# Splitting the first two experts' biases ahead of time, and moving the first norm's scale and shift into the first expert's product

## The chip, the cores and the metric

The kernel runs on one core of one Trainium2 chip. The metric is the device time of one execution, in microseconds (us). A core has five engines that run their own instruction streams in order: PE (matrix products), DVE (vector), ACT (activation), POOL and SP (which here only issues DMAs). Sixteen DMA engines move data between HBM and the on-chip memory.

## The reference, cut to what matters

One layer: an RWKV-7 time mixer, a norm, a mixture of 32 experts with four of them per token, a second norm, a gated per-layer input, a third norm. 256 tokens, width 1024, all in float32. The part around the change:

```
x = layer_norm(ALPHA * x + mixed, ln_mix_g, ln_mix_b)         # first norm: scale g, shift b
logits = x @ router_w + router_b;  top 4 of 32, softmax        # router
h = x_e @ w_gu[e] + b_gu[e]                                    # 1024 -> 2048, for each expert e
act = min(h[:F], 7) * sigmoid(1.702 * ...) * (clip(h[F:]) + 1)
y_e = act @ w_down[e] + b_down[e]                              # 1024 -> 1024
x = layer_norm(ALPHA * x + sum of gated y_e, ln_ffn_g, ln_ffn_b)
```

Each expert has 8 MB of `w_gu` and 4 MB of `w_down`, so the experts read 403 MB of weights.

## The kernel before

**Stages.** `rwkv` (the mixer), `route` (first norm without its scale and shift, router, one-hot matrices, gathering of the first two experts' tokens into `xg0`), `overflow` (four products that clear the output sums `acc`, and a branch that all engines take together), `experts`, `tail`.

**The ring.** Expert weights stream through a ring of eleven 2 MB tiles. A plan lists them in order: for each pair of experts eight `gu` tiles (four an expert, two of eight k steps each), then four `d` tiles. Eleven are issued before the experts begin. After that `ring.free` puts the next load of the plan into a tile as soon as PE has read it for the last time; SP issues these loads in that order (L128 for `gu`, L139 for `d`).

**Order of the experts.** For pair b: `gu(2b)`, `gu(2b+1)` (products `ph`, L1215, then the bias, L1222), `combine` of the pair before, `tr` (transposes, L1235), `gates`, for even b `gather` (products `pg`, L1188, for the next four experts), `down` (`pd`, L1263). PE's order is that of the code between `step()` calls and the scheduler's inside one; DVE's and ACT's order is the scheduler's throughout. `bank` hands out four PSUM banks for all of these products.

**The biases.** `biases` loads all 32 experts' biases in six pieces of 512 columns, each into 96 rows of a scratch tile (three copies of 32 rows, L1049), and splits each into three bf16 parts in `B3`: two casts on ACT (L1051, L1053), two subtractions (L1052, L1054) and a cast (L1055) on DVE. A one-column selector then adds expert e's bias to a sum with one matmul for each 512 columns.

**First norm's scale and shift.** `residual`, between `gu(0)` and `gu(1)`, spreads g and b over the partitions with four matmuls (`pgb`, L1200), applies them to `x1` on DVE (L1202), and adds ALPHA * x1 to `acc` with the matrix `scaled` (L1204).

Of the kernel before, what the change touches and what calls it, by code (L numbers as in the profile page):

```python
# [16 lines left out]
OP = mybir.AluOpType  # L17
# [154 lines left out]
def consts(tc, pool):  # L172
    nc = tc.nc
    c = {}
    ident = pool.tile([128, 128], F32, name="ident")
    nc.gpsimd.memset(ident, 1.0)
    nc.gpsimd.affine_select(ident, ident, pattern=[[1, 128]], compare_op=OP.is_equal, fill=0.0,
                            base=0, channel_multiplier=-1)
    c["ident"] = ident
    identr = pool.tile([128, 128], F32R, name="identr")  # L180
    nc.scalar.copy(identr, ident)
    c["identr"] = identr
    upto = pool.tile([128, 128], F32, name="upto")
    nc.gpsimd.memset(upto, 1.0)
    nc.gpsimd.affine_select(upto, upto, pattern=[[1, 128]], compare_op=OP.is_ge, fill=0.0,
                            base=0, channel_multiplier=-1)
    c["upto"] = upto
    ones = pool.tile([128, 128], F32, name="ones")
    nc.gpsimd.memset(ones, 1.0)
    c["ones"] = ones  # L190
    iota = pool.tile([128, CAP], F32, name="iota")
    nc.gpsimd.iota(iota, pattern=[[1, CAP]], base=1, channel_multiplier=0, allow_small_or_imprecise_dtypes=True)
    c["iota"] = iota
    scaled = pool.tile([128, 128], F32, name="scaled")
    nc.gpsimd.tensor_scalar(scaled, ident, ALPHA, None, op0=OP.mult)
    c["scaled"] = scaled
    return c


# [801 lines left out]
class Moe:  # L1001
    def __init__(self, tc, keep, c, A, x1):
        self.tc, self.c, self.A, self.x1 = tc, c, A, x1
        self.gate = keep.tile([128, 2, E], F32, name="gate")
        self.pos = keep.tile([128, 2, E], F32, name="pos")
        self.cnt = keep.tile([128, E + 1], I32, name="cnt")
        self.pm = keep.tile([128, 2, KC], F32, name="pm")

    def first(self, pool):

# [3 lines left out]
    def prepare(self, RP, ps):  # L1014
# [6 lines left out]
        for i, nm in enumerate(["ln_mix_g", "ln_mix_b"]):  # L1021
# [14 lines left out]
        nc.vector.scalar_tensor_tensor(rw, pc[:, 0:E][:, None, :].to_broadcast([128, KC, E]), -1.0 / D, rw,  # L1036
                                       op0=OP.mult, op1=OP.add)

    def biases(self, W, scratch):

        nc, A, ident = self.tc.nc, self.A, self.c["ident"]
        B3 = W.tile([96, 3 * D], BF, name="B3")
        sel3 = W.tile([96, E], BF, name="sel3")
        n = 512
        for i, bf in enumerate(scratch):
            bf = bf[0:96]
            src = A["moe_b_gu"] if i * n < 2 * D else A["moe_b_down"]
            cols = i * n % (2 * D)
            nc.sync.dma_start(bf, bass.AP(tensor=src.tensor, offset=src.offset + cols, ap=[[0, 3], [src.shape[-1], E], [1, n]]))  # L1049
            o = B3[:, i * n:i * n + n]  # L1050
            nc.scalar.copy(o, bf)  # L1051
            nc.vector.tensor_sub(bf[0:64], bf[0:64], o[0:64])  # L1052
            nc.scalar.copy(o[0:64], bf[0:64])  # L1053
            nc.vector.tensor_sub(bf[32:64], bf[32:64], o[32:64])  # L1054
            nc.vector.tensor_copy(o[32:64], bf[32:64])  # L1055
        for r in range(3):
            rs = slice(32 * r, 32 * r + 32)
            nc.gpsimd.tensor_scalar(sel3[rs, :], ident[rs, rs], 1.0, 0.0, op0=OP.mult, op1=OP.add)
        return B3, sel3

    def route(self, RP, psA, psB, psI, sums):

# [72 lines left out]
    def experts(self, ring):  # L1135
# [4 lines left out]
        with ExitStack() as ctx:  # L1140
# [24 lines left out]
            def bank(name):  # L1165
                return PS.tile([128, 512], F32, name=name, tag="m", bufs=4)

            def one(e):
                return sel3[:, e:e + 1].to_broadcast([96, CAP])

            def batch(e):

# [5 lines left out]
            def gather(e):  # L1178
# [4 lines left out]
                for q in range(KC // 2):  # L1183
# [6 lines left out]
                    copy = nc.vector.tensor_copy if q % 2 else nc.scalar.copy  # L1190
                    copy(xq[:, 2 * q:2 * q + 2, 0:n * CAP], pg[:, :, 0:n * CAP])

            def residual():

                for i, op in enumerate((OP.mult, OP.add)):
                    for h in range(2):
                        hs = slice(512 * h, 512 * h + 512)
                        pb = bank("pgb")
                        r = 32 * h
                        nc.tensor.matmul(pb, ident[r:r + 2, r + i:r + i + 1].to_broadcast([2, 128]), rows[h], start=True, stop=True)  # L1200
                        for cp in range(2):
                            nc.vector.tensor_tensor(x1[cp][:, hs], x1[cp][:, hs], pb, op=op)  # L1202
                            if i:
                                nc.tensor.matmul(acc[cp][h], c["scaled"], x1[cp][:, hs], start=False, stop=False,  # L1204
                                                 skip_group_check=True)

            def gu(e):
                xg, _, i = batch(e)
                ph = [bank(f"ph{n}") for n in range(2)]
                for k in range(KC):  # L1210
                    w = ring["gu", e, k // 2]
                    for n in range(2):
                        for h in range(2):
                            o = n * D + h * 512
                            pe(nc.tensor.matmul(ph[n][64 * h:64 * h + 64, :], xg[:, k, i * CAP:i * CAP + CAP],  # L1215
                                                w[:, k % 2, o:o + 512], start=k == 0, stop=False))
                    if k % 2:
                        ring.free(("gu", e, k // 2))
                for n in range(2):
                    for h in range(2):  # L1220
                        o = n * D + h * 512
                        pe(nc.tensor.matmul(ph[n][64 * h:64 * h + 64, :], one(e), B3[:, o:o + 512], start=False, stop=True))  # L1222
                step()
                s = act[e % 2]
                nc.vector.tensor_scalar(g, ph[0], 7.0, None, op0=OP.min)  # L1225
                nc.vector.tensor_scalar(l, ph[1], 7.0, -7.0, op0=OP.min, op1=OP.max)
                nc.scalar.activation(s, g, AF.Sigmoid, scale=1.702)  # L1227
                nc.vector.scalar_tensor_tensor(l, l, 1.0, g, op0=OP.add, op1=OP.mult)
                nc.vector.tensor_mul(s, s, l)
# [20 lines left out]
            def down(b):  # L1250


                pd = [bank(f"pd{h}") for h in range(2)]
                for i in range(2):
                    e = 2 * b + i
                    side = [slice(64 * (i ^ h), 64 * (i ^ h) + 64) for h in range(2)]
                    for h in range(2):
                        o = 2 * D + 512 * h
                        pe(nc.tensor.matmul(pd[h][side[h], :], one(e), B3[:, o:o + 512], start=True, stop=False))  # L1259
                    for fh in range(2):  # L1260
                        for k in range(4):
                            for h in range(2):
                                pe(nc.tensor.matmul(pd[h][side[h], :], actT[:, i, k, 64 * fh:64 * fh + 64],  # L1263
                                                    ring["d", e, fh][:, k, 512 * h:512 * h + 512],
                                                    start=False, stop=fh == 1 and k == 3))
                        ring.free(("d", e, fh))
                    step()
                nc.scalar.copy(ob[:, 0], pd[0])  # L1268
                for i in range(2):
                    nc.vector.tensor_copy(ob[64 * i:64 * i + 64, 1], pd[1][64 - 64 * i:128 - 64 * i])  # L1270
# [5 lines left out]
                                            start=False, stop=2 * b == E - 2, skip_group_check=True))  # L1276
                    step()

            rows = [act[1][32 * h:32 * h + 2] for h in range(2)]
            for h in range(2):  # L1280
                for i, nm in enumerate(["ln_mix_g", "ln_mix_b"]):
                    nc.sync.dma_start(rows[h][i:i + 1], self.A[nm][:, 512 * h:512 * h + 512])
            B3, sel3 = self.biases(W, [ob[:, 0], ob[:, 1], g, l] + [xq[:, 2 * i:2 * i + 2].rearrange("p a b -> p (a b)") for i in range(2)])
            ring.rest()
            for b in range(E // 2):
                gu(2 * b)
                if not b:
                    residual()
                gu(2 * b + 1)
                if b:  # L1290
                    combine(b - 1)
                self.ready(ring, bank, b - READY, pe)
                step()
                tr(2 * b)
                pgt = gates(b)
                nc.vector.tensor_copy(GT, pgt[:, 0:T])
                if b % 2 == 0 and b < E // 2 - 1:
                    gather(2 * b + 2)
                    step()
                tr(2 * b + 1)  # L1300
                down(b)
# [237 lines left out]
```

## Time and profile before

| | |
|---|---|
| median of 3 runs | 1335.9 us (1335.29 to 1336.46) |
| the profiled execution's own time | 1339.56 us |
| its span, first to last instruction | 1337.9 us |
| PE busy | 1213.4 us (91%) |
| DVE, ACT, POOL busy | 440.4, 216.8, 178.3 us |
| mean granted TensorE clock | 0.952 of full speed |
| mean DMA traffic | 323 GB/s |

The stages lie in the span so: the mixer and `route` to 346 us, the experts from 347 to 1289 us, the tail to 1338 us. "Share" in DMA columns is the mean busy share of the 16 DMA engines; "<-" names what an engine waited for.

### The profile page before, as it was taken

How to read it: one execution, taken by the hardware profiler on the slowest of the kernel's cores; microseconds unless marked ns; L12 is line 12 of the kernel's file. 1: busy time of each engine (PE TensorE's matmuls, PEld its weight loads, DVE VectorE, ACT ScalarE, POOL GpSimd, SP SyncE). 2: the span in 40 equal slices, each digit the busy share in tenths (PEclk: the TensorE clock that was granted, in tenths of full speed). 3: DMA queues.
4: the chain of work that ended last, by engine and by line, in shares of the span. 5: the costliest groups of instructions: out<-in, count | busy, mean ns of one | idle time of the engine just before them, and what ended most of it. 6: DMA issues, size and time to landing. Idle time of an engine off the chain costs nothing.

```text
span 1337.9 us, 14931 instructions
## 1 busy us (share of the span) xinstructions
PE 1213.4 (91%) x5983; PEld 693.4 (52%) x5984; DVE 440.4 (33%) x1080; ACT 216.8 (16%) x459; POOL 178.3 (13%) x308
## 2 busy tenths in 40 slices
PE   6988888988789999999988988999899989989996
PEld 5666666776326545645634432554255345525642
DVE  5886879885231112111102011111111111101235
ACT  3544434441211001000000000101010010101001
POOL 9465646530000000000000000000000000000000
PEclk9987879896879999999999999999999999999988
DMA  7331101475469999999999899999999999999951
GB/s 223 100 109 32 33 1 49 161 319 214 155 270 387 426 427 430 427 428 428 427 428 427 358 428 429 428 427 428 429 428 427 427 427 427 429 427 427 422 204 32
DMA packets 41806, 431.57 MB, mean 323 GB/s; under 512 B 5507, under 2 KB 10043, under 8 KB 17284
## 3 DMA queue, kind: packets, MB, share of 16 engines
q1 hardware_dynamic: 41412, 430.04, 77.9%
q8 instruction: 49, 0.80, 0.2%
q10 hardware_dynamic: 320, 0.52, 0.1%
q14 instruction: 25, 0.20, 0.0%
HBM read 429.50 MB, written 1.05 MB: 322 GB/s over the span
## 4 chain that ended last, share of the span: by engine, by line
PE 49%; DMA 23%; DVE 1%; SPq 0%; ACT 0%; issue 0%; DVEq 0%
DMA ring_f<-in_moe_w_gu 18%; PE ph L1215 18%; PE pd L1263 16%; PE pg L1188 5%; PE acc L1275 4%; DMA ring_f<-in_moe_w_down 3%; PE tpg L1459 2%; DMA xq<-in_moe_b_down 1%; PE ptr L1235 1%; PE ph L1222 1%; PE pd L1259 1%; PE pn L1333 1%; PE ppq L1324 1%; SPq L1049 0%; PE tpg L1430 0%; PE acc L1204 0%
## 5 line engine op out<-in xcount | busy, mean ns | idle before, releaser
L1215 PE MATMUL ph<-ring_f,xq 128*64 128x512 f32 x1920 | 431.5, 594 | 44.2 <-DMA ring_f<-in_moe_w_gu 44.2
L1215 PEld LDWEIGHTS ph<-ring_f,xq 128*64 128x64 f32 x1920 | 204.4, 137 | 256.1 <-issue 119.1
L1263 PE MATMUL pd<-ring_f,xg 128*64 128x512 f32 x1024 | 251.0, 595 | 0.0
L1263 PEld LDWEIGHTS pd<-ring_f,xg 128*64 128x64 f32 x1024 | 105.8, 137 | 126.5 <-issue 112.3
L1225 DVE TENSOR_SCALAR g<-ph 128x512 f32<-128x512 f32 x32 | 22.1, 692 | 428.4 <-PE ph L1222 428.4
L1270 DVE COPY ob<-pd 64x512 f32<-64x512 f32 x32 | 22.0, 688 | 250.8 <-PE pd L1263 250.5
L1227 ACT ACTIVATE s<-g 128x512 f32<-128x512 f32 x32 | 20.2, 630 | 469.1 <-DVE g L1225 469.1
L1188 PE MATMUL pg<-oh,x 128*128 128x256 f32 (+1 forms) x256 | 63.4, 406 | 0.0
L1188 PEld LDWEIGHTS pg<-oh,x 128*128 128x128 f32 x256 | 62.0, 336 | 0.0
L1275 PE MATMUL acc<-ob,oh 128*128 128x512 f32 x128 | 59.2, 605 | 0.7 <-ACT ob L1268 0.7
L1268 ACT COPY ob<-pd 128x512 f32<-128x512 f32 x16 | 9.4, 587 | 244.6 <-PE pd L1263 244.6
L368 POOL TENSOR_TENSOR w_lo<-w_raw,w_hi 128x512 fp32r<-128x512 f32 (+2 forms) x32 | 41.3, 1292 | 15.7 <-ACT w_hi L351 15.6
L1275 PEld LDWEIGHTS acc<-ob,oh 128*128 128x128 f32 x128 | 23.0, 189 | 30.8 <-issue 28.7
L351 ACT CAST w_hi<-w_raw 128x1024 fp32r<-128x1024 f32 x32 | 33.2, 1048 | 33.6 <-issue 14.8
L1222 PE MATMUL ph<-B,sel 96*64 96x512 bf16 x128 | 29.5, 385 | 7.9 <-DVE B L1055 7.9
L1215 PE MATMUL ph<-ring_f,xg 128*64 128x512 f32 x128 | 32.4, 653 | 3.7 <-PEq L1349 3.7
L370 DVE TENSOR_TENSOR w_lo<-w_raw,w_hi 128x512 fp32r<-128x512 f32 (+2 forms) x32 | 29.6, 926 | 6.9 <-ACT w_hi L351 6.8
L1459 PE MATMUL tpg<-ring_f,x 128*128 128x512 f32 x64 | 29.9, 627 | 0.0
L1237 ACT COPY xg<-ptr 128x512 f32<-128x512 f32 x32 | 18.8, 586 | 64.6 <-PE ptr L1235 63.5
L1222 PEld LDWEIGHTS <-sel 96*64 96x64 bf16 x128 | 11.2, 111 | 28.6 <-issue 16.4
L1235 PEld LDWEIGHTS ptr<-ident,s 128*128 128x128 f32 x128 | 19.4, 208 | 8.4 <-issue 8.2
L1215 PEld LDWEIGHTS ph<-ring_f,xg 128*64 128x64 f32 x128 | 10.5, 151 | 25.1 <-issue 19.5
(365 smaller groups left out, 1489.2 us busy)
## 6 DMA issues: line engine op xcount, KB each, us to landing
ring_f<-in_moe_w_gu SPq DMA_DIRECT2D x128, 2048.0 KB
ring_f<-in_moe_w_down SPq DMA_DIRECT2D x62, 2048.0 KB
w_raw<-in_rwkv_w_rkv SPq DMA_DIRECT2D x24, 512.0 KB
w_raw<-in_rwkv_w_o SPq DMA_DIRECT2D x8, 512.0 KB
ring_f<-in_moe_w_down SPq DMA_DIRECT2D x8, 512.0 KB
ring_f<-in_ple_w_gate SPq DMA_DIRECT2D x8, 512.0 KB
x<-in_x SPq DMA_DIRECT2D x4, 256.0 KB
ring_f<-in_ple_w_proj SPq DMA_DIRECT2D x1, 1024.0 KB
```

The costliest lines, as they stand in the source:

```text
L351: eng.copy(out, in_)
L368: nc.gpsimd.tensor_sub(lw[:, D - g:], raw[:, D - g:], hi.bitcast(F32)[:, D - g:])
L370: nc.vector.tensor_sub(lw[:, 0:D - g], raw[:, 0:D - g], hi.bitcast(F32)[:, 0:D - g])
L1188: pe(nc.tensor.matmul(pg[:, k, 0:n * CAP], lhs, oh[:, cp, 0:n].rearrange("p a b -> p (a b)"), start=cp == 0, stop=cp == 1))
L1215: pe(nc.tensor.matmul(ph[n][64 * h:64 * h + 64, :], xg[:, k, i * CAP:i * CAP + CAP], w[:, k % 2, o:o + 512], start=k == 0, stop=False))
L1222: pe(nc.tensor.matmul(ph[n][64 * h:64 * h + 64, :], one(e), B3[:, o:o + 512], start=False, stop=True))
L1225: nc.vector.tensor_scalar(g, ph[0], 7.0, None, op0=OP.min)
L1235: pe(nc.tensor.transpose(pt[:, k, :], av[:, k, :], ident))
L1263: pe(nc.tensor.matmul(pd[h][side[h], :], actT[:, i, k, 64 * fh:64 * fh + 64], ring["d", e, fh][:, k, 512 * h:512 * h + 512], start=False, ...
L1270: nc.vector.tensor_copy(ob[64 * i:64 * i + 64, 1], pd[1][64 - 64 * i:128 - 64 * i])
L1275: pe(nc.tensor.matmul(acc[cp][h], GT[:, cp * 128:cp * 128 + 128], ob[:, h], start=False, stop=2 * b == E - 2, skip_group_check=True))
L1459: i = nc.tensor.matmul(pg[cp][h], xt[cp][:, k, :], ring["wg", k // 4][:, k % 4, halves[h]], start=False, stop=k == KC - 1)
```

## The change

A small tile `B0` is filled in `prepare`, during the mixer: the first two experts' biases, cut into 24 rows of 256 columns, three copies, split into three parts by the same five operations (now the function `parts`). The norm's g and b go into 16 rows of 128 columns (`rows`) at the same place. In the experts, `shift` adds the bias from `B0` for experts 0 and 1 (two matmuls of 256 columns for each 512), and from `B3` for the others. `B3` is filled from the same six loads as before, but they are issued by ACT and not by SP, and into other scratch (`xq` four times, `ob` twice). `scale(n)`, four times, stands in `gu(0)` behind each second k step: four matmuls of 128 columns into a bank `pgb`, then two DVE operations on `x1`. `residual` keeps only the products into `acc`, and stands behind `gu(1)`. The tile `ones` becomes a broadcast column of `iota`; `scaled` is written over `upto` just before the experts.

```diff
+        raw = RP.tile([128, D], F32, name="w_raw", bufs=3)[0:96, 0:256]
+        nc.gpsimd.memset(raw, 0.0)
+        for r in range(3):
+            nc.sync.dma_start(raw[32 * r:32 * r + 16], A["moe_b_gu"][0][0:2].rearrange("e (n q) -> (e n) q", q=256))
+            nc.sync.dma_start(raw[32 * r + 16:32 * r + 24], A["moe_b_down"][0][0:2].rearrange("e (n q) -> (e n) q", q=256))
+        self.parts(self.B0[0:96], raw)
...
-            nc.sync.dma_start(bf, bass.AP(tensor=src.tensor, offset=src.offset + cols, ap=[[0, 3], [src.shape[-1], E], [1, n]]))
...
+            nc.scalar.dma_start(bf, bass.AP(tensor=src.tensor, offset=src.offset + cols, ap=[[0, 3], [src.shape[-1], E], [1, n]]))
+            self.parts(B3[:, i * n:i * n + n], bf)
...
+            def shift(out, e, o, start, stop):
+
+                if e < 2:
+                    parts = [(8 * e + o // 256 + j if o < 2 * D else 8 + 4 * e + o // 256 + j, self.B0[0:96], 256 * j) for j in range(2)]
+                else:
+                    parts = [(e, B3[:, o:o + 512], 0)]
+                for i, (r, b, at) in enumerate(parts):
+                    pe(nc.tensor.matmul(out[:, at:at + b.shape[-1]], self.sel3[0:96, r:r + 1].to_broadcast([96, CAP]), b,
+                                        start=start and not i, stop=stop and i == len(parts) - 1, skip_group_check=e < 2))
...
+            def scale(n):
+
+                i, h = divmod(n, 2)
+                hs = slice(512 * h, 512 * h + 512)
+                pb = bank("pgb")
+                for j in range(4):
+                    r = 8 * i + 4 * h + j
+                    pe(nc.tensor.matmul(pb[:, 128 * j:128 * j + 128], ident[0:16, r:r + 1].to_broadcast([16, 128]), self.rows[0:16],
+                                        start=True, stop=True))
+                for cp in range(2):
+                    nc.vector.tensor_tensor(x1[cp][:, hs], x1[cp][:, hs], pb, op=(OP.mult, OP.add)[i])
...
                     if k % 2:
                         ring.free(("gu", e, k // 2))
+                        if not e:
+                            step()
+                            scale(k // 2)
+                            step()
...
             for b in range(E // 2):
                 gu(2 * b)
-                if not b:
-                    residual()
                 gu(2 * b + 1)
                 if b:
                     combine(b - 1)
+                else:
+                    residual()
```

PE before, from the last quarter of `gu(0)` to the start of `gu(1)` (`ph` is `gu`'s sum, `ring_2_f` the fourth weight tile, `B` is `B3`):

```order
L1215 MATMUL ph_4242<-ring_2_f,xg_84 64x512 x2
L1215 MATMUL ph_4243<-ring_2_f,xg_84 64x512 x2
L1222 LDWEIGHTS sel_4201
L1222 MATMUL ph_4242<-B_4200,sel_4201 64x512
L1200 MATMUL pgb<-s_4195,ident 128x512
...
L1222 MATMUL ph_4243<-B_4200,sel_4201 64x512
L1200 MATMUL pgb<-s_4195,ident 128x512 x2
L1215 MATMUL ph_4309<-ring_3_f,xg_84 64x512 x4
```

PE after the change, from the third `scale` group on (the first two stand behind `ring_f` and `ring_0_f`; L1238 is the old L1215, `B_75` is `B0`):

```order
L1238 MATMUL ph_4253<-ring_1_f,xg_83 64x512 x2
L1217 MATMUL pgb<-rows,ident 128x128 x4
L1238 MATMUL ph_4252<-ring_2_f,xg_83 64x512 x2
L1238 MATMUL ph_4253<-ring_2_f,xg_83 64x512 x2
...
L1217 MATMUL pgb<-rows,ident 128x128 x4
L1185 LDWEIGHTS sel_76
L1185 MATMUL ph_4252<-B_75,sel_76 64x256
...
L1238 MATMUL ph_4331<-ring_3_f,xg_83 64x512 x4
```

The bias matmuls of `gu(0)` no longer read the large split, and the four `pgb` groups have moved from behind `gu(0)` into it.

DVE after the change, from the fifth and sixth pieces of the large split (in `ob`) to the start of `gu(0)`'s activation (L1053, L1055, L1056 are the subtractions and the cast of `parts`, L1220 is `scale`'s operation on `x1`, L1251 the activation's first):

```order
L1053 TENSOR_TENSOR ob<-ob,B_4214 64x512
L1055 TENSOR_TENSOR xq<-xq,B_4214 32x512
L1056 CAST B_4214<-xq 32x512
L1055 TENSOR_TENSOR ob<-ob,B_4214 32x512
L1220 TENSOR_TENSOR x_0_68<-x_0_68,pgb 128x512
L1220 TENSOR_TENSOR x_1_69<-x_1_69,pgb 128x512
L1056 CAST B_4214<-xq 32x512
L1055 TENSOR_TENSOR ob<-ob,B_4214 32x512
L1056 CAST B_4214<-ob 32x512 x2
L1220 TENSOR_TENSOR x_0_68<-x_0_68,pgb 128x512
...
L1251 TENSOR_SCALAR g<-ph_4252 128x512
```

The first operation on a `pgb` bank stands behind the subtractions of all six pieces of the large split, as L1202 did before the change.

ACT after the change, right behind the branch (L1067 are the six loads, L1052 and L1054 the casts of `parts`):

```order
L1067 DMA xq<-in_moe_b_gu 96x1x512 x4
L1052 ACT_TABLE_LOAD
L1052 CAST B_4214<-xq 96x512 x2
L1067 DMA ob<-in_moe_b_down 96x1x512
L1052 CAST B_4214<-xq 96x512
L1067 DMA ob<-in_moe_b_down 96x1x512
L1054 CAST B_4214<-xq 64x512
```

Four loads are issued at once, the fifth behind the second piece's cast and the sixth behind the third's. SP's queue loses its ten loads there, and begins with the ring's next tile.

## Rows read from the trace of the kernel before

**Rows 1.** The page: DMA packets by size, and two kinds of issues.

```profile
DMA packets 41806, 431.57 MB, mean 323 GB/s; under 512 B 5507, under 2 KB 10043, under 8 KB 17284
...
ring_f<-in_moe_w_gu SPq DMA_DIRECT2D x128, 2048.0 KB
...
ob<-in_moe_b_gu SPq DMA_DIRECT2D x2, 192.0 KB
```

**Rows 2.** Windows: stretch, its length, engines' busy us, PEclk, DMA share, GB/s.

```profile
355.00:359.00 4.00, 4.00 (x20) 1.40 (x18) 1.37 (x2) 2.11 (x3) 0.00 (x0) 1.00 0.20 76
360.00:371.00 11.00, 4.84 (x19) 1.40 (x16) 4.77 (x8) 3.24 (x6) 0.00 (x0) 0.83 1.00 272
372.00:383.00 11.00, 7.29 (x14) 2.02 (x14) 10.42 (x19) 3.95 (x6) 0.00 (x0) 0.50 1.01 427
384.00:390.00 6.00, 6.00 (x24) 2.01 (x21) 0.00 (x0) 0.00 (x0) 0.00 (x0) 0.97 0.19 82
391.00:395.00 4.00, 4.00 (x17) 1.25 (x17) 0.00 (x0) 0.00 (x0) 0.00 (x0) 1.00 0.00 0
...
415.00:419.00 4.00, 4.00 (x17) 1.41 (x15) 0.00 (x0) 0.00 (x0) 0.00 (x0) 1.00 0.29 70
419.00:640.00 221.00, 221.00 (x999) 123.95 (x999) 35.65 (x62) 15.01 (x25) 0.00 (x0) 1.00 1.01 427
...
750.00:1280.00 530.00, 494.69 (x2164) 243.48 (x2162) 74.19 (x127) 38.90 (x66) 0.00 (x0) 1.00 1.01 427
```

**Rows 3.** Timeline of ACT at the start of the experts: start, us, what, [idle before].

```profile
354.59 1.28 ACT L1051 ACT_TABLE_LOAD   x1 [12.34 <-DMA ob<-in_moe_b_gu]
...
357.17 0.62 ACT L1051 CAST B<-ob 96x512 bf16<-96x512 f32 x1 [0.66 <-DMA ob<-in_moe_b_gu]
359.83 0.62 ACT L1051 CAST B<-g 96x512 bf16<-96x512 f32 x1 [2.04 <-DMA g<-in_moe_b_gu]
...
371.86 0.62 ACT L1051 CAST B<-xq 96x512 bf16<-96x512 f32 x1 [3.00 <-DMA xq<-in_moe_b_down]
```

**Rows 4.** Timeline of SP's issues, several stretches.

```profile
348.09 1.65 SPq L1049 DMA_DIRECT2D ob<-in_moe_b_gu  x2
...
353.50 2.62 SPq L1049 DMA_DIRECT2D xq<-in_moe_b_down  x1
356.23 2.36 SPq L139 DMA_DIRECT2D ring_f<-in_moe_w_down  x1
...
394.14 0.33 SPq L128 DMA_DIRECT2D ring_f<-in_moe_w_gu  x1
...
417.17 0.33 SPq L128 DMA_DIRECT2D ring_f<-in_moe_w_gu  x1
```

**Rows 5.** Timeline of PE: the first expert's product.

```profile
347.19 15.45 PE L1215 MATMUL ph<-ring_f,xg 128*64 128x512 f32 x64 [3.69 <-PEq L1349]
```

**Rows 6.** The chain that ended last, in order of time: start, us, what.

```profile
353.50 18.34 DMA xq<-in_moe_b_down
...
373.91 0.34 DVE B L1055
...
376.49 0.69 DVE x L1202
...
380.50 8.10 PE ph L1215 x26
388.60 3.63 PE acc L1204 x8
...
402.30 7.78 PE pg L1188 x32
410.08 0.47 PE ptr L1235 x4
410.55 0.33 PE pd L1259
...
475.17 13.73 PE ph L1215 x64
```

More of the change, by code (lines that the diff above doesn't have):

```diff
@@ L187, in consts @@
     c["upto"] = upto
-    ones = pool.tile([128, 128], F32, name="ones")
-    nc.gpsimd.memset(ones, 1.0)
-    c["ones"] = ones
     iota = pool.tile([128, CAP], F32, name="iota")
@@ L193, in consts @@
     c["iota"] = iota
-    scaled = pool.tile([128, 128], F32, name="scaled")
-    nc.gpsimd.tensor_scalar(scaled, ident, ALPHA, None, op0=OP.mult)
-    c["scaled"] = scaled
+    c["ones"] = iota[:, 0:1].to_broadcast([128, 128])
     return c
@@ L1007, in __init__ @@
         self.pm = keep.tile([128, 2, KC], F32, name="pm")
+        self.rows = keep.tile([128, 128], F32, name="rows")
+        self.B0 = keep.tile([128, 256], BF, name="B0")
+        self.sel3 = keep.tile([128, E], BF, name="sel3")
     def first(self, pool):
@@ L1037, in prepare, with parts @@
                                        op0=OP.mult, op1=OP.add)
+        for i, nm in enumerate(["ln_mix_g", "ln_mix_b"]):
+            nc.sync.dma_start(self.rows[8 * i:8 * i + 8], A[nm][0].rearrange("(c q) -> c q", q=128))
+        raw = RP.tile([128, D], F32, name="w_raw", bufs=3)[0:96, 0:256]
[4 more added lines that the diff above has]
+        self.parts(self.B0[0:96], raw)
+        for r in range(3):
+            rs = slice(32 * r, 32 * r + 32)
+            nc.gpsimd.tensor_scalar(self.sel3[rs, :], self.c["ident"][rs, rs], 1.0, 0.0, op0=OP.mult, op1=OP.add)
+    def parts(self, o, bf):
+        nc = self.tc.nc
+        nc.scalar.copy(o, bf)
+        nc.vector.tensor_sub(bf[0:64], bf[0:64], o[0:64])
+        nc.scalar.copy(o[0:64], bf[0:64])
+        nc.vector.tensor_sub(bf[32:64], bf[32:64], o[32:64])
+        nc.vector.tensor_copy(o[32:64], bf[32:64])
     def biases(self, W, scratch):
-        nc, A, ident = self.tc.nc, self.A, self.c["ident"]
+        nc, A = self.tc.nc, self.A
         B3 = W.tile([96, 3 * D], BF, name="B3")
-        sel3 = W.tile([96, E], BF, name="sel3")
         n = 512
@@ L1048, in biases @@
             cols = i * n % (2 * D)
-            nc.sync.dma_start(bf, bass.AP(tensor=src.tensor, offset=src.offset + cols, ap=[[0, 3], [src.shape[-1], E], [1, n]]))
[L1050 to L1059, printed above, removed]
+            nc.scalar.dma_start(bf, bass.AP(tensor=src.tensor, offset=src.offset + cols, ap=[[0, 3], [src.shape[-1], E], [1, n]]))
+            self.parts(B3[:, i * n:i * n + n], bf)
+        return B3
     def route(self, RP, psA, psB, psI, sums):
@@ L1166, in bank @@
                 return PS.tile([128, 512], F32, name=name, tag="m", bufs=4)
-            def one(e):
-                return sel3[:, e:e + 1].to_broadcast([96, CAP])
+            def shift(out, e, o, start, stop):
[6 more added lines that the diff above has]
+                                        start=start and not i, stop=stop and i == len(parts) - 1, skip_group_check=e < 2))
             def batch(e):
@@ L1191, in gather @@
                     copy(xq[:, 2 * q:2 * q + 2, 0:n * CAP], pg[:, :, 0:n * CAP])
+            def scale(n):
[8 more added lines that the diff above has]
+                    nc.vector.tensor_tensor(x1[cp][:, hs], x1[cp][:, hs], pb, op=(OP.mult, OP.add)[i])
             def residual():
-                for i, op in enumerate((OP.mult, OP.add)):
+                for cp in range(2):
                     for h in range(2):
[L1197 to L1205, printed above, removed]
+                        pe(nc.tensor.matmul(acc[cp][h], scaled, x1[cp][:, 512 * h:512 * h + 512], start=False, stop=False,
+                                            skip_group_check=True))
+                step()
             def gu(e):
@@ L1215, in gu @@
                             pe(nc.tensor.matmul(ph[n][64 * h:64 * h + 64, :], xg[:, k, i * CAP:i * CAP + CAP],
-                                                w[:, k % 2, o:o + 512], start=k == 0, stop=False))
+                                                w[:, k % 2, o:o + 512], start=k == 0, stop=False, skip_group_check=e < 2))
                     if k % 2:
                         ring.free(("gu", e, k // 2))
+                        if not e:
+                            step()
+                            scale(k // 2)
+                            step()
                 for n in range(2):
                     for h in range(2):
-                        o = n * D + h * 512
-                        pe(nc.tensor.matmul(ph[n][64 * h:64 * h + 64, :], one(e), B3[:, o:o + 512], start=False, stop=True))
+                        shift(ph[n][64 * h:64 * h + 64, :], e, n * D + h * 512, False, True)
                 step()
@@ L1257, in down @@
                     for h in range(2):
-                        o = 2 * D + 512 * h
-                        pe(nc.tensor.matmul(pd[h][side[h], :], one(e), B3[:, o:o + 512], start=True, stop=False))
+                        shift(pd[h][side[h], :], e, 2 * D + 512 * h, True, False)
                     for fh in range(2):
@@ L1264, in down @@
                                                     ring["d", e, fh][:, k, 512 * h:512 * h + 512],
-                                                    start=False, stop=fh == 1 and k == 3))
+                                                    start=False, stop=fh == 1 and k == 3, skip_group_check=e < 2))
                         ring.free(("d", e, fh))
@@ L1277, in combine @@
                     step()
[L1279 to L1283, printed above, removed]
+            scaled = c["upto"]
+            nc.gpsimd.tensor_scalar(scaled, ident, ALPHA, 0.0, op0=OP.mult, op1=OP.add)
+            B3 = self.biases(W, [xq[:, 2 * i:2 * i + 2].rearrange("p a b -> p (a b)") for i in range(4)] + [ob[:, 0], ob[:, 1]])
             ring.rest()
```

## The prediction

> **What bounds the kernel now.** I read the windows first, for DMA traffic against time. From 419 us on the sixteen DMA engines stay at a share of 1.00 and 427 GB/s, and 750 to 1280 us looks the same [rows 2]. A 2048 KB tile of the ring [rows 1] takes 2.097 MB / 427 GB/s = 4.9 us. So from 419 us the weight stream sets the end. If that stream becomes continuous some us earlier or later, the end moves by the same amount. Two holes lie just ahead: nothing moves from 391 to 395 us, and the share is 0.29 from 415 to 419 us [rows 2]. In both, no ring tile is free, since PE is late. SP's issues show the releases: the first tile of `gu(1)` is refilled at 394.14 us, the first `d` tile at 417.17 us [rows 4]. The second ends the last hole. So the time hangs on when PE gets through `gu(0)`, `gu(1)` and into `down(0)`.
>
> The chain of waits says what holds PE there. The matmuls of `gu(0)` take 347.19 to 362.64 us [rows 5], but `gu(1)` starts at 380.50 us; between them the chain runs through 18.34 us of waiting for the last piece of the bias load, then the splits, then `residual` [rows 6]. ACT's timeline gives the landings: pieces 1, 2, 3 at 354.6, 357.2 and 359.8 us, the sixth at t = 371.86 us [rows 3]. The kernel's clock at the transition is t: `gu(1)` starts at t + 8.6, `down(0)` (410.55) at t + 38.7, and its first tile is free at t + 45.3.
>
> **Why the landing is slow.** While only bias pieces move, the DMA share is 0.20 and 76 GB/s [rows 2], three engines' worth out of sixteen. Pieces of 192 KB land 2.66 us apart [rows 3], 64 KB an engine, 24 KB/us each. Once the ring's tiles join in, total traffic is only 272 GB/s at a share of 1.00 up to 371 us, against 427 right after the last piece has landed; and from 384 to 390 us 0.19 is left over [rows 2], which I read as the same three engines finishing their parts of four ring tiles (128 KB each of a tile). Those three thus moved 6 x 64 + 4 x 128 = 896 KB in the 40 us from 350 to 390, 22.4 KB/us.
>
> **The change, part by part.** (1) Bias of experts 0 and 1 from `B0`: the four bias matmuls of `gu(0)` lose their wait. Sixteen small ones replace eight; as each has half the columns, I cost them at nothing, at most 0.3 us a product.
>
> (2) `scale` in `gu(0)`. Its four `pgb` groups need a bank each, and of four banks `ph` holds two. The third group must wait until DVE has read the first group's bank. In DVE's order that reading (L1220) stands behind the subtractions of all six pieces of the large split. So PE stops after three quarters of `gu(0)`, at about 347.2 + 12 + 1 = 360.2 us, until the sixth piece has landed and been split. The wait is not gone; it has moved from the bias matmul to a PSUM bank. Queued behind it on PE are the last quarter of `gu(0)`, whose tile can't be freed, and all of `gu(1)`.
>
> From the landing t': a cast (0.62 [rows 3]), then on DVE, in its order, an L1053, an L1055, an L1056 (0.34), an L1055 and two L1220 (0.69 [rows 6], and so much for the subtractions too), 4.4 us in all; then PE, at half clock after the pause (PEclk 0.50 in 372 to 383 us [rows 2]): a `scale` group (0.47 at full clock by four such transposes [rows 6], 0.9 here), eight matmul instructions (3.4 us at full clock, 4.9 with the first at half), the last group 0.5, the biases 1.0. That is t' + 11.8 for `gu(1)`, 3.2 later than before relative to the landing. `gu(1)` itself then loses its slow start and the products into `acc` in its middle: 13.73 + 1.0 + 3.63 + transposes 0.7 + 7.78 + 0.47 = 27.3 us [rows 6], against 410.55 - 380.50 = 30.1 before. `down(0)` starts at t' + 39.1: 0.4 us later relative to the landing. So **shift = (t' - 371.9) + 0.4.**
>
> (3) The loads go to ACT's queue. Before, the six pieces were ahead of the ring's tiles in SP's queue: the next tile was issued at 356.23, when all six were out [rows 4]. Now SP issues that tile when `gu(0)` frees it, at about 352.3 us, and two more at about 356.3 and 360.2. ACT is past the branch at 347, so the first piece leaves 1 us earlier than at 348.09 [rows 4], and lands at about 353.5. From there the three engines have five pieces, 320 KB each, and three tiles, 384 KB each, in two queues at once. Shared evenly, the pieces are through when 640 KB are: 26 us at 24 KB/us, 28.6 us at 22.4 KB/us, that is t' = 379.5 to 382. I take 381. The bounds: below, pieces at the undisturbed 2.66 us, with the sixth issued behind the third's cast: 366.8; above, all 704 KB first, 353.5 + 31.4 = 385.
>
> The Trainium skill speaks against this part: "DMA: Bandwidth & Descriptors", section "Issuing engines are not separate DMA queues", says that DMAs from different engines run on the same sixteen DMA engines and interleave, so that a second issuer saves only issue time. By it the move buys SP's issue time (1.65 us for the first two pieces [rows 4]) and no transfer time; no run here shows it yet.
>
> (4) Work moved into the mixer: six small loads, one memset, three selector columns, two casts and three DVE operations, half as wide as those of 0.62 and 0.34 to 0.69 us [rows 3, 6]: between 0 and about 1.5 us if all of it lay on the path, and DVE waits enough there; I take 0.3. The schedule of the mixer's second half is reordered on all engines; a swap costs at most an instruction (0.3 to 0.7 us), and a handful of them 2 to 3 us either way; I take 0. The matrices `ones` and `scaled` cost nothing.
>
> Sum: 381 - 371.9 + 0.4 + 0.3 = **+9.8 us**. On the profiled execution's 1339.56 us that gives 1349.4; that execution is 3.7 us above the median, so I forecast 1335.9 + 9.8 = 1345.7 us.
>
> **Rivals.** *Pieces last.* If an engine with two queues alternates packet by packet, a ring packet counts for more than a bias packet: 24,522 packets of the page are over 8 KB [rows 1], about 16 KB each for 403 MB, where a bias row is 2 KB. The tiles then go first and the pieces land at the end, t' = 382 to 385: +12.3, 1348. For it: large packets; against: nothing in this trace has two loaded queues. The skill's same page, section "Queues, rings and completion order", states such turns by packet; if a packet is one row, this rival is what it gives, and no run here shows it.
>
> *Pieces first.* The pieces land 4.1 us apart, as pieces 4 to 6 did before beside the ring's tiles ((371.86 - 359.83) / 3 = 4.0 [rows 3]): t' = 373, +1.8, 1337.7. For it: that was the cadence under load; against: there the pieces were ahead in the one queue.
>
> *Faster.* The bias queue is undisturbed: t' = 366.8, -4.4, 1331.5. It decides for faster once t' is below 368.8. For it: three engines carry few ring bytes before 356; against: the 272 GB/s of 360 to 371 us [rows 2].
>
> *PE is not held at all*, because DVE in fact reads `pgb` earlier: its order excludes that.
>
> **Chances.** Shared evenly 0.42, pieces last 0.23, pieces first 0.20, faster 0.11, the mixer's new order deciding by more than 3 us 0.04. A difference under 0.2% (2.7 us) can't be told from none. Slower: 0.42 and 0.23 almost whole, a third of pieces first: 0.71. Same: the rest of that, and edges: 0.15. Faster: 0.14. Range: from between faster and pieces first (1332.5) up to pieces last with 2 us of the mixer (1350.5). The likeliest case alone: 1342.5 to 1348.
>
> **What would show it.** In the new profile PE should wait some 20 us between the second and third `pgb` groups, released by DVE at L1220; ACT's casts (L1052) should show the sixth piece after 379 us; the DMA share should not fall to 0.20 early, as ring tiles flow from 354 us; `down(0)` should start near 420 us, and the traffic be continuous from about 429 us. I am wrong if the sixth piece lands before 374 us, or if PE passes the third group before it.

## The result, and the profile after

| | median | runs |
|---|---|---|
| before, in the same comparison | 1334.47 us | 1331.15 to 1336.46 (6) |
| after | 1345.86 us | 1344.71 to 1346.82 (6) |

The ratio is 1.0087, 95% interval 1.0072 to 1.0102: 0.87% slower, 11.4 us. The profiled execution of the changed kernel took 1344.71 us, its span 1343.0. Its experts start at 341.48 us, those of the profile before at 347.19 [rows 5]. So from here on I count from the experts' start, the first matmul of `gu(0)`. From there to the end of the span it is 1337.9 - 347.2 = 990.7 us before and 1343.0 - 341.5 = 1001.5 after: +10.8.

PE's timeline after the change, from the experts' start to `down(0)` (columns as in rows 5):

```profile
341.48 5.17 PE L1238 MATMUL ph<-ring_f,xg 128*64 128x512 f32 x16 [3.64 <-PEq L1372]
346.58 1.15 PE L1217 MATMUL pgb<-rows,ident 16*128 16x128 f32 x8
...
352.33 3.65 PE L1238 MATMUL ph<-ring_f,xg 128*64 128x512 f32 x16
381.41 2.04 PE L1217 MATMUL pgb<-rows,ident 16*128 16x128 f32 x8 [25.43 <-DVE x L1220]
383.38 6.40 PE L1238 MATMUL ph<-ring_f,xg 128*64 128x512 f32 x16
389.71 1.15 PE L1217 MATMUL pgb<-rows,ident 16*128 16x128 f32 x8
390.79 0.63 PE L1185 MATMUL ph<-B,sel 96*64 96x256 bf16 x8
391.25 13.96 PE L1238 MATMUL ph<-ring_f,xg 128*64 128x512 f32 x64
...
418.14 0.41 PE L1185 MATMUL pd<-B,sel 96*64 96x256 bf16 x2
```

The one long wait, 25.43 us, is where the prediction put it: at the third `pgb` group, released by DVE at L1220. The biases of `gu(0)` (L1185, at 390.79) wait for nothing now. What follows the wait is slow: the 16 matmuls at 383.38 take 6.40 us, the 16 at 352.33 took 3.65.

ACT's timeline, the casts that follow each landing (as rows 3):

```profile
349.88 0.62 ACT L1052 CAST B<-xq 96x512 bf16<-96x512 f32 x1 [0.78 <-DMA xq<-in_moe_b_gu]
...
365.88 0.62 ACT L1052 CAST B<-xq 96x512 bf16<-96x512 f32 x1 [15.38 <-DMA xq<-in_moe_b_gu]
371.63 0.62 ACT L1052 CAST B<-xq 96x512 bf16<-96x512 f32 x1 [4.37 <-DMA xq<-in_moe_b_gu]
374.31 0.62 ACT L1052 CAST B<-ob 96x512 bf16<-96x512 f32 x1 [1.54 <-DMA ob<-in_moe_b_down]
376.97 0.62 ACT L1052 CAST B<-ob 96x512 bf16<-96x512 f32 x1 [1.52 <-DMA ob<-in_moe_b_down]
```

The second piece lands 8.4 us after the experts' start, the third only 16 us later, the last two 2.66 us apart again. The sixth lands 35.5 us after the start; before it was 371.86 - 347.19 = 24.7 [rows 3, 5].

SP's queue, and the windows (as rows 4 and 2):

```profile
346.68 0.34 SPq L139 DMA_DIRECT2D ring_f<-in_moe_w_down  x1
351.36 4.99 SPq L128 DMA_DIRECT2D ring_f<-in_moe_w_gu  x2
```

```profile
350.00:362.00 12.00, 5.98 (x32) 2.17 (x27) 0.68 (x1) 0.50 (x1) 0.00 (x0) 0.84 1.00 370
366.00:376.00 10.00, 0.00 (x0) 0.00 (x0) 4.08 (x7) 3.39 (x6) 0.00 (x0) 0.50 0.19 74
378.00:390.00 12.00, 8.59 (x26) 3.79 (x27) 7.37 (x14) 2.42 (x4) 0.00 (x0) 0.54 0.01 2
...
422.00:424.00 2.00, 2.00 (x11) 0.85 (x11) 0.00 (x0) 0.00 (x0) 0.00 (x0) 1.00 0.02 8
425.00:640.00 215.00, 215.00 (x973) 121.68 (x971) 34.46 (x60) 14.40 (x24) 0.00 (x0) 1.00 1.01 427
```

Three ring tiles are issued while the pieces are on their way. From 350 to 362 us they fill the engines; from 366 to 376 only three engines' worth is busy (share 0.19), at first still with the last 0.20 MB of the tiles and then with the pieces alone; from 378 to 390 nothing moves, since PE stands. The traffic is continuous from 425 us. The tail of PE's wait, by the chain:

```profile
343.35 22.51 DMA xq<-in_moe_b_gu
...
365.88 11.06 DMA ob<-in_moe_b_down
...
379.98 1.29 DVE x L1220 x2
```

The third piece alone is 22.51 us of it; it is also what holds up the sixth, which ACT issues behind the third's cast.

How the two queues share the engines shows in the DMA queues of 352 to 362 us (packets, MB, share of 16 engines' time; q1 is SP's queue, q10 ACT's):

```profile
DMA packets 296, 3.77 MB, mean 377 GB/s; under 512 B 30, under 2 KB 30, under 8 KB 71
q1 hardware_dynamic: 254, 3.69, 96.7%
q10 hardware_dynamic: 42, 0.08, 2.4%
```

30 of the packets are of 4 bytes. The 225 over 8 KB are SP's, 3.69 MB / 225 = 16.4 KB each; the other 41 are ACT's rows of 2 KB. On sixteen engines SP's 225 are 14 an engine; on three ACT's 41 are 14 as well. The queues take turns packet by packet: the trace has ACT's packets in threes, nearly all of them 0.74 to 0.80 us apart, and a large one of SP's takes 0.69 us on average. As a packet of SP's is 16 KB and one of ACT's 2 KB, the pieces get about a ninth of those three engines until the tiles are through.

### The profile page after: what moved, and what is told of

It is laid out like the page before. It is cut to its first block, busy times and chain, and to the rows that moved or that the text cites. A ratio compares the mean times of both kernels' runs of the same rounds, so it can differ in the third digit from the quotient of the medians.

```text
span 1343.0 us, 15011 instructions
## 1 busy us (share of the span) xinstructions
PE 1200.4 (89%) x6019; PEld 696.5 (52%) x6020; DVE 444.1 (33%) x1083; ACT 218.0 (16%) x461; POOL 177.4 (13%) x308
## 4 chain that ended last, share of the span: by engine, by line
PE 49%; DMA 24%; DVE 1%; ACTq 0%; ACT 0%; issue 0%; DVEq 0%; SPq 0%
DMA ring_f<-in_moe_w_gu 19%; PE ph L1238 18%; PE pd L1288 15%; PE pg L1205 5%; PE acc L1300 4%; DMA ring_f<-in_moe_w_down 3%; PE tpg L1482 2%; DMA xq<-in_moe_b_gu 2%; PE ptr L1261 1%; DMA ob<-in_moe_b_down 1%; PE ph L1185 1%; PE pd L1185 1%; PE pn L1356 1%; PE ppq L1347 1%; PE acc L1226 0%; PE pgt L1272 0%
## 5 line engine op out<-in xcount | busy, mean ns | idle before, releaser
L1238 PE MATMUL ph<-ring_f,xq 128*64 128x512 f32 x1920 | 431.5, 594 | 45.2 <-DMA ring_f<-in_moe_w_gu 45.1
L1238 PEld LDWEIGHTS ph<-ring_f,xq 128*64 128x64 f32 x1920 | 204.9, 137 | 257.0 <-issue 118.1
L1288 PEld LDWEIGHTS pd<-ring_f,xg 128*64 128x64 f32 x1024 | 109.0, 136 | 120.8 <-issue 105.9
L1251 DVE TENSOR_SCALAR g<-ph 128x512 f32<-128x512 f32 x32 | 22.1, 692 | 423.2 <-PE ph L1185 423.2
L363 POOL TENSOR_TENSOR w_lo<-w_raw,w_hi 128x512 fp32r<-128x512 f32 (+2 forms) x32 | 40.8, 1280 | 17.5 <-ACT w_hi L346 16.3
L1238 PE MATMUL ph<-ring_f,xg 128*64 128x512 f32 x128 | 32.8, 669 | 3.6 <-PEq L1372 3.6
L365 DVE TENSOR_TENSOR w_lo<-w_raw,w_hi 128x512 fp32r<-128x512 f32 (+2 forms) x32 | 32.3, 1009 | 8.6 <-ACT w_hi L346 8.5
L1185 PEld LDWEIGHTS <-sel 96*64 96x64 bf16 x204 | 17.2, 110 | 22.5 <-issue 16.5
L1217 PE MATMUL pgb<-rows,ident 16*128 16x128 f32 x32 | 5.5, 320 | 25.4 <-DVE x L1220 25.4
L1185 PE MATMUL ph<-B,sel 96*64 96x512 bf16 (+1 forms) x136 | 26.4, 367 | 0.0
```

Source lines behind the costliest of these rows:

```text
L363: nc.gpsimd.tensor_sub(lw[:, D - g:], raw[:, D - g:], hi.bitcast(F32)[:, D - g:])
L365: nc.vector.tensor_sub(lw[:, 0:D - g], raw[:, 0:D - g], hi.bitcast(F32)[:, 0:D - g])
L1185: pe(nc.tensor.matmul(out[:, at:at + b.shape[-1]], self.sel3[0:96, r:r + 1].to_broadcast([96, CAP]), b, start=start and not i, stop=stop a ...
```

## The experiments

The table gives, for each profile: the experts' start, and after it the cast of the sixth piece, `gu(1)`, `down(0)` and the end of the span; then the median and the ratio to the kernel before on the same chip. (The first row is the profile of before, "after" that shown above.)

| kernel | start | sixth | gu(1) | down(0) | end | median | ratio (95%) |
|---|---|---|---|---|---|---|---|
| before | 347.2 | 24.7 | 33.3 | 63.3 | 990.7 | | |
| before_again | 342.4 | 24.4 | 33.0 | 63.1 | 990.4 | 1334.53 (1 run) | |
| after | 341.5 | 35.5 | 49.8 | 76.7 | 1001.5 | 1345.86 | 1.0087 (1.0072 to 1.0102) |
| after_again | 343.0 | 35.4 | 49.8 | 76.7 | 1001.5 | 1346.14 (1 run) | |
| e2, loads by SP | 344.1 | 23.6 | 36.7 | 63.6 | 990.0 | 1333.88 | 0.9998 (0.9985 to 1.0011) |
| e3, before with loads by ACT | 342.4 | 40.1 | 47.5 | 77.3 | 1004.3 | 1349.78 | 1.0122 (1.0102 to 1.0141) |
| e1, splits behind | 342.6 | 54.8 | 20.5 | 75.0 | 1001.4 | 1347.23 | 1.0098 (1.0080 to 1.0116) |
| e4, spread, by ACT | 341.3 | 25.7 | 29.9 | 58.7 | 984.4 | 1329.36 | 0.9971 (0.9956 to 0.9987) |
| e5, spread, behind, by ACT | 342.6 | 21.4 | 20.6 | 47.5 | 973.8 | 1318.23 | 0.9879 (0.9861 to 0.9897) |
| e8, spread, by SP | 343.1 | 11.1 | 21.0 | 47.9 | 974.2 | 1318.38 | 0.9880 (0.9862 to 0.9898) |
| e9, spread, behind, by SP | 341.6 | 10.9 | 20.9 | 47.8 | 974.0 | 1317.27 | 0.9872 (0.9854 to 0.9889) |
| e10, before, spread | 345.2 | 11.3 | 22.8 | 52.7 | 979.7 | 1321.52 | 0.9898 (0.9882 to 0.9915) |

In all twelve, from `down(0)` to the end it is 924.8 to 927.4 us. So the start of `down(0)`, counted from the experts' start, does set the time, and each experiment can be read there.

My theory was the prediction's: the pieces land late since they are in a queue beside the ring's, and PE waits for DVE, which waits for the pieces. The main rivals: the small products and banks cost by themselves; or the wait for a bank is what costs, and the landing doesn't matter.

**before_again and after_again: both kernels once more, unchanged.**

> The kernel before, profiled once more. Theory (the experts started 5.8 us earlier in the changed kernel's profile since the mixer's length differs from one execution to the next): the experts start at 341 to 345 us in this one, the sixth piece lands 25 us after that, down(0) starts 63 us after it, and the span is some 990 us longer than the start. Rival (the new order of the mixer saves these 5.8 us): they start at 347 us again.

> The changed kernel, profiled once more. Theory: whenever the experts start (341 to 345 us), the third piece lands some 24 us after it and the sixth some 36, and down(0) starts some 77 us after it. Rival (the long wait for the third piece was a chance of one execution): the pieces land evenly, or 5 us or more off these.

The kernel before starts its experts at 342.41 us here, and everything behind that is as it was:

```profile
342.41 15.36 PE L1215 MATMUL ph<-ring_f,xg 128*64 128x512 f32 x64 [3.54 <-PEq L1349]
```

```profile
366.84 0.62 ACT L1051 CAST B<-xq 96x512 bf16<-96x512 f32 x1 [2.93 <-DMA xq<-in_moe_b_down]
```

The changed kernel's third piece is cast at 363.94 - 342.99 = 21.0 us after the start (24.4 in the other profile, where I expected 24), its sixth at 35.4. The theory holds in both: the mixer's length goes with the execution, and the late third and sixth piece come again. From 100 to 150 us the first profile of before has a granted clock of 0.85, this one 0.93, the one after the change 0.93. Over all profiles the start lies at 342.4 to 347.2 us with the old mixer (four) and 341.3 to 344.1 with the new (eight).

**e2: the loads by SP again.**

```diff
-            nc.scalar.dma_start(bf, bass.AP(...))
+            nc.sync.dma_start(bf, bass.AP(...))
```

> The changed kernel, with the six bias loads issued by SP ahead of the ring's tiles, as before the change. Theory (the loss is the late landing of the pieces, and PE's wait for a bank follows the landing): the sixth piece lands some 25 us after the experts' start instead of 36, down(0) starts some 64 us after it instead of 77, and the time is that of the kernel before within 3 us, 1335. Rival (the small products in gu(0) and the wait for a bank cost by themselves, whatever the landing): most of the loss stays, 1342 or more.

The time is that of the kernel before. PE still stands at the third `pgb` group, for 12.15 us:

```profile
372.11 2.04 PE L1217 MATMUL pgb<-rows,ident 16*128 16x128 f32 x8 [12.15 <-DVE x L1220]
```

All the rest of the change, put together, is worth nothing that these runs can tell (the interval is 1.7 us either way) while the pieces land at 24 us; the loss is the queue's.

**e3: the kernel before, with the loads by ACT.**

```diff
-            nc.sync.dma_start(bf, bass.AP(...))
+            nc.scalar.dma_start(bf, bass.AP(...))
```

> The kernel before, with one word changed: the six bias loads are issued by ACT and not by SP. Theory (the queue alone makes the loss): the sixth piece lands some 35 us after the experts' start, gu(1) and down(0) start about 10 us later relative to it, and the time is 1342 to 1347. Rival (the loss needs the wait for a bank of the changed kernel): the bias matmuls only come later under cover, 1334 to 1337.

The theory holds, and the loss is larger than I expected, 15.5 us; `gu(1)` and `down(0)` start 14 us later and not 10:

```profile
362.85 0.62 ACT L1051 CAST B<-g 96x512 bf16<-96x512 f32 x1 [10.92 <-DMA g<-in_moe_b_gu]
377.30 0.62 ACT L1051 CAST B<-l 96x512 bf16<-96x512 f32 x1 [13.07 <-DMA l<-in_moe_b_gu]
```

Here `gu(0)` runs through, so SP also issues its fourth tile (at 362.89 us, right as the third piece lands, 5.0 us after PE is through with `gu(0)`), and the three engines must bring 128 KB more each before the pieces are through: 6 x 64 + 4 x 128 = 896 KB in the 40.5 us from the first issue (342.05) to the last cast (382.51), 22 KB/us, the rate of the prediction. In the changed kernel it was 768 KB in 35.8 us, 21.4 KB/us.

**e1: DVE's splits ordered behind the norm's operations.** PE is not held in `gu(0)` then.

```diff
+        i = nc.vector.tensor_sub(bf[0:64], bf[0:64], o[0:64])
+        if last:
+            self.behind(i, last)
...
-            self.parts(B3[:, i * n:i * n + n], bf)
...
+                    self.split(B3, scratch, scaled_last[-1])
                     residual()
```

`split` calls `parts` for the six pieces, and `scaled_last` holds the DVE operations of `scale`.

> The changed kernel, with DVE's subtractions of the large split ordered behind the last operation on the first norm's scale and shift; loads and queue as changed. Theory (PE is held only since the reading of a pgb bank stands behind those subtractions in DVE's order): PE passes the third pgb group without a pause, gu(1) starts some 20 us after the experts' start instead of 50, and the pause that is left is for the first activation behind the splits, up to some 42 us after the start. The stream becomes continuous 10 to 20 us earlier: 1326 to 1336. Rival (the weight tiles come no earlier, since three DMA engines still carry the pieces, and PE only waits elsewhere, for a tile): no gain, 1343 to 1348.

The rival's time was right, and my expectation of 1326 to 1336 fell; but PE's wait is for an activation and not for a tile, as the rival had it. PE passes all four groups and starts `gu(1)` 20.5 us after the start, and yet the time is that of the changed kernel (1001.4 us from the start, against 1001.5):

```profile
363.11 13.96 PE L1245 MATMUL ph<-ring_f,xg 128*64 128x512 f32 x64
...
407.06 1.10 PE L1268 MATMUL ptr<-ident,s 128*128 128x128 f32 x4 [25.93 <-DVE s L1262]
```

```profile
383.07 0.62 ACT L1052 CAST B<-xq 96x512 bf16<-96x512 f32 x1 [15.77 <-DMA xq<-in_moe_b_gu]
...
397.39 0.62 ACT L1052 CAST B<-ob 96x512 bf16<-96x512 f32 x1 [10.41 <-DMA ob<-in_moe_b_down]
```

```profile
352.00:370.00 18.00, 18.00 (x99) 7.82 (x99) 6.34 (x10) 3.04 (x4) 0.00 (x0) 1.00 1.00 393
...
404.00:424.00 20.00, 16.94 (x70) 12.68 (x71) 8.91 (x20) 2.86 (x5) 0.00 (x0) 0.84 0.00 1
```

As PE goes on, it frees four more tiles in that time, seven in all, and these hold the pieces back until 397.39 us: 6 x 64 + 7 x 128 = 1280 KB an engine in the 55.1 us from the first issue, 23.2 KB/us. ACT's sixth load is out at 361.12 us here, behind no cast, and still lands 36 us later; so the issue behind the third's cast isn't what makes the pieces late. Then the first activation, queued on DVE and ACT behind the splits, is what PE waits for: 25.93 us again. From 404 to 424 us nothing moves. The two queues also held up each other's issues: ACT stood 13.74 us in the issue of its sixth load, and SP issued three tiles at 383.11, 386.40 and 397.44 us, each within 0.05 us of one of the last three casts (383.07, 386.37 and 397.39), though PE was through with `gu(1)` at 377.07. Why a tile's load waits for a piece, no run here shows.

**e4: each piece as three loads of 32 rows**, still by ACT.

```diff
-            nc.scalar.dma_start(bf, bass.AP(..., ap=[[0, 3], [src.shape[-1], E], [1, n]]))
+            for r in range(3):
+                nc.scalar.dma_start(bf[32 * r:32 * r + 32], bass.AP(..., ap=[[src.shape[-1], E], [1, n]]))
```

> The changed kernel, with each piece of 96 rows loaded by three DMAs of 32 rows, so that the outermost dimension of a load is 32 and not 3. Theory (a load whose outermost dimension is 3 goes over three of the sixteen DMA engines, and these three are what is slow): the pieces use all engines, the sixth lands some 14 to 20 us after the experts' start, PE waits a few us at the third pgb group, and the time falls to 1318 to 1328. Rival (the pieces are late since they take turns with the ring's large packets, however they are spread): they still land 30 us after the start or later, 1340 to 1346.

The time is 4.9 us under that of before and 16.5 under the 1345.86 of the changed kernel, but 1.4 us above the range that I gave (the twelve runs go from 1325.88 to 1335.96). The first four pieces are cast by 352.26 us, 11 us after the start; the last two come late, the sixth at 25.7 us and not at 14 to 20:

```profile
352.26 0.62 ACT L1052 CAST B<-xq 96x512 bf16<-96x512 f32 x1
360.11 0.62 ACT L1052 CAST B<-ob 96x512 bf16<-96x512 f32 x1 [7.23 <-DMA ob<-in_moe_b_down]
...
367.05 0.62 ACT L1052 CAST B<-ob 96x512 bf16<-96x512 f32 x1 [4.95 <-DMA ob<-in_moe_b_down]
```

The queues of 352 to 362 us show why:

```profile
q1 hardware_dynamic: 214, 3.24, 86.1%
q10 hardware_dynamic: 198, 0.27, 8.0%
```

ACT's 198 packets stand beside SP's 214, both on sixteen engines now: the trace has sixteen packets of 4 bytes for each of these loads, and three for each load of the changed kernel. These are turns by packet again, but at 1.4 KB against 15 (the packets of 4 bytes counted in). So both theories hold a part: spread loads are quick alone, and still lose to the tiles where they meet them. PE waits twice, not at the third group but 4.47 us at the fourth and 3.02 ahead of `gu(1)`. (DVE's order differs from the changed kernel's here too: the first two operations on `x1` stand ahead of the fifth piece.)

**e5: e4 and e1 together** (both edits as above).

> The changed kernel, with the spread loads of e4 and the splits ordered behind the norm's operations as in e1; loads by ACT. Theory (in e4 PE was held, at the fourth pgb group and at the start of gu(1), only since DVE's operations on the banks stood behind the splits of the fifth and sixth piece): gu(1) starts 20 us after the experts' start instead of 30, the splits are through by the end of gu(1), and the time is 1317 to 1323. Rival (with gu(0) and gu(1) run without a pause, the weight tiles keep the pieces back still longer, and the first activation waits for them): gain lost, 1327 or more.

As expected by the theory, 1318.23 us. `gu(1)` starts 20.6 us after the start, and the sixth piece at 21.4 is early enough for the activation.

**e8: e4 with the loads by SP, ahead of the ring's tiles. e9: e8 and e1 together.**

```diff
-                nc.scalar.dma_start(bf[32 * r:32 * r + 32], bass.AP(...))
+                nc.sync.dma_start(bf[32 * r:32 * r + 32], bass.AP(...))
```

> The changed kernel, with the spread loads of e4, issued by SP ahead of the ring's tiles. Theory (in e4 the first four pieces landed within 11 us of the experts' start and only the last two were kept back by the tiles): with all six ahead of the tiles they land within some 15 us of the start, PE waits 5 us or less at the pgb groups, and the time is 1317 to 1323. Rival (18 issues of some 0.4 us put the first weight tile off, or the tiles of the ring are late anyway): no better than e4, 1327 to 1331.

> As e8, with the splits ordered behind the norm's operations as in e1 too. Theory: gu(1) starts 20 us after the experts' start, nothing of the large split lies on the path any more, down(0) starts some 48 us after the start, and the time is 1316 to 1321. Rival (the traffic of the ring's tiles is the limit by then): as e8, within 2 us.

Both land in their ranges. In e9, while the pieces move and after:

```profile
344.00:350.00 6.00, 6.00 (x30) 2.57 (x28) 1.28 (x2) 3.15 (x5) 0.00 (x0) 0.89 0.46 140
352.00:372.00 20.00, 20.00 (x109) 8.46 (x108) 12.27 (x20) 5.82 (x9) 0.00 (x0) 1.00 1.00 412
394.00:396.00 2.00, 2.00 (x12) 0.71 (x10) 0.00 (x0) 0.00 (x0) 0.00 (x0) 1.00 0.02 8
398.00:430.00 32.00, 32.00 (x154) 20.29 (x153) 4.05 (x6) 1.22 (x2) 0.00 (x0) 1.00 1.01 429
```

The pieces move at a share of 0.46 and 140 GB/s, against 0.20 and 76 [rows 2], and PE has no hole. e8 is within 1.1 us of e9 and the intervals overlap, so ordering the splits shows no effect once the pieces land at 11 us; as e9's rival said. Both beat both kernels: e9 by 1.28% that of before.

**e10: the kernel before, with the loads spread, by SP.** The edit is in the old `biases`:

```diff
-            nc.sync.dma_start(bf, bass.AP(..., ap=[[0, 3], [src.shape[-1], E], [1, n]]))
+            for r in range(3):
+                nc.sync.dma_start(bf[32 * r:32 * r + 32], bass.AP(..., ap=[[src.shape[-1], E], [1, n]]))
```

> The kernel before, with its six bias loads spread as in e8 and issued by SP; B0 and the moved norm are not in it. Theory (the landing of the pieces is all that made gu(1) late, and what the change takes off gu(0) is only worth the rest of residual between gu(0) and gu(1)): the six pieces land within some 15 us of the experts' start, down(0) starts some 53 us after the start, against 48 in e9, and the time is 1320 to 1326. Rival (without B0 and the moved norm PE still waits some 10 us or more between gu(0) and gu(1)): 1327 to 1334.

1321.52 us, as the theory had it: the landing alone gives back 13 of the 17 us that e9 gains.

```profile
362.28 1.13 PE L1201 MATMUL pgb<-s,ident 2*128 2x512 f32 x4
...
364.78 3.27 PE L1201 MATMUL pgb<-s,ident 2*128 2x512 f32 x4 [0.82 <-DVE x L1203]
367.98 8.07 PE L1216 MATMUL ph<-ring_f,xg 128*64 128x512 f32 x26
```

`down(0)` starts 52.7 us after the start, 4.9 later than in e9 and 4.8 later than in e8, which leaves the order of the splits alone; by the profiles that is what the small tile and the moved norm are worth once nothing else is in the way. The medians are 4.2 us apart (e9) and 3.1 (e8), on different chips, and the intervals of the ratios overlap (0.9854 to 0.9889 and 0.9862 to 0.9898 against 0.9882 to 0.9915), so the size of this gain rests on the profiles.

## Why the prediction was right, step by step

The forecast was 1345.7 us, the median is 1345.86. It rested on four steps.

- **What is held, and by whom** was right: e2 and e3 show that the queue makes the whole loss, and the wait moved from the biases to a bank that DVE frees behind all six pieces. The rival that PE is not held is out. e1 adds that this wait isn't the limit by itself: without it, the first activation waits for the same pieces. Nor is the move to ACT's queue a matter of issue time alone: it makes the pieces land 10.8 us later.
- **The landing** was forecast 33.8 us after the experts' start (381 - 347.2) and came at 35.5 and 35.4. But of the two cases, *shared evenly* was the likeliest and *pieces last* is what happened. The step "five pieces and three tiles in two queues at once, shared evenly" failed: the queues share by packets, 14 to 14 an engine, not by bytes, and the sixth piece came 1.7 us later than forecast. That costs the forecast little, since the sixth piece is through only when nearly all of the pieces and tiles on those three engines are, whichever go first; *pieces last* gave 34.8 to 37.8 us. (640 KB at 24 KB/us are 26.7 us and not 26, which leaves 381 inside the case.) The Trainium skill's page "DMA: Bandwidth & Descriptors", section "Queues, rings and completion order", has these turns by packet, and both queue counts above agree.
- **From the landing to `gu(1)`** I counted 11.8 us (the parts add up to 11.7) and it took 14.3 (376.97 to 391.25). DVE's part is right, 4.4 us up to 381.41. PE's was sized too small: the third group took 2.0 us to the next matmuls and not 0.9, the 16 matmuls 6.3 and not 4.9, the last group 1.1 and not 0.5; the biases were 0.5 shorter. A group is eight matmuls in the trace, where the four transposes that I took its price from are four: at full clock it takes 1.08 us (346.58 to 347.66), not 0.47. And the granted clock was 0.54 over 378 to 390 us, so that nearly all of the 16 matmuls ran at half clock and not only the first half. From `gu(1)` to `down(0)` I counted 27.3 and it took 26.9. So `down(0)` came 76.7 us after the experts' start, where I had 420 - 347.2 = 72.8.
- **From `down(0)` to the end** I took no change, and it became 2.6 us shorter (927.42 to 924.86). 1.1 us of that is common to the kernels with the new order in `down(0)` (926.2 to 926.4 in e1, e2, e5, e8, e9). Of the other 1.5, 1.2 lies in the tail: from the first of SP's last eight loads (1278.79 us) to the end it is 64.2 us, against 65.4 to 65.5 in e1, e2 and e9. Two groups of products there take 3.69 and 8.15 us, at a mean granted clock of 0.88 over 17 to 31 us behind that load, where e2 has 4.39 and 8.90 us at 0.76. Why the clocks differ stays open.

Counted from the experts' start: landing +10.8 (forecast 9.1), from there to `down(0)` +2.6 (forecast 0.4), from there to the end -2.6 (0): +10.8, and 11.4 by the medians, where the forecast had 9.8 with 0.3 for the mixer. That it met the time within 0.2 us is luck: the 2.2 us that were missing ahead of `down(0)` are made up for by the 2.6 behind it, and the median that it started from, 1335.9, is 1.4 us above that of the longer comparison. The mixer's 0.3 us can't be seen; its start scatters by 5 us.

## What to carry to other kernels

A wait that is taken off one instruction goes to the next thing that needs the same late work: ask which instruction stands behind it in each engine's queue, and what the freed engine releases meanwhile (in e1 more tiles, which made the late load later still). A small load that others wait for should go out ahead of the bulk traffic in the same queue, and over all DMA engines; here loads with an outermost dimension of 32 in place of 3 were worth 13 us even in the kernel before (e10). A change whose main part shows nothing (e2) can still be worth something once the true limit is gone (by the profiles, `down(0)` 4.8 us earlier in e8 than in e10).

## What the runs showed of the hardware

- Two queues on the same DMA engines alternated by packet, at 2 KB against 16 and at 1.4 against 15: 41 packets of ACT's on three engines beside 225 of SP's on sixteen, 198 beside 214 on sixteen each. A queue of 2 KB rows thus had some 2.4% of sixteen engines' time, where three engines are 19%.
- A load of 96 rows written as 3 x 32 moves at a share of 0.19 to 0.20 and 74 to 77 GB/s, as three loads of 32 rows, issued by SP one behind the other, at 0.46 and 140 GB/s (e9). The same page of the Trainium skill, section "Rules for kernel authors", says that an outermost dimension under 16, such as a leading broadcast of a few copies, confines a DMA to at most as many engines; the shares, and three packets of 4 bytes for each load, agree with three.
- After its stop of 25 us PE ran at a granted clock of 0.50 (1.2 GHz) from 380 to 388 us, and the 16 matmuls of a quarter of `gu(0)` took 6.40 us instead of 3.65, a `pgb` group 2.04 instead of 1.15: the pause cost 3.6 us beyond its length.
